# Spreading the later adaLN products of one decoder block over more of its mixer stage

## The chip, the cores and the metric

The kernel runs on one core of one Trainium2 chip. The metric is device time in microseconds (us), from runs of the whole kernel; lower is better. Each engine of the core (TensorE, called PE in the profile; VectorE, DVE; ScalarE, ACT; GpSimd, POOL; and SyncE, SP, which here only issues transfers) works through its own list of instructions in the order in which that list was written.

## The reference

The computation is one decoder block on 512 tokens of width 2048. A vector `c` gives six modulation vectors, two token mixers (eight pairs of RWKV-7 heads and four causal pooling groups) read one projection, their outputs are projected back, and a gated MLP with a short convolution follows. Cut to what matters here:

```python
c_act = silu(c)
mod = c_act @ w_ada + b_ada                       # 2048 x 12288: adaLN
sh1, sc1, gt1, sh2, sc2, gt2 = split(mod, 6)
h = rmsnorm(x, norm1_g) * (1 + sc1) + sh1
p = h @ w_in
y_rwkv = rwkv7_mixer(p[..., :3360], ...)          # 16 heads of 64, delta rule
y_pool = pool_mixer(p[..., 3360:], ...)           # windows 2, 4, 8, 16
x = x + gt1 * (concat(y_rwkv, y_pool) @ w_out)
h = rmsnorm(x, norm2_g) * (1 + sc2) + sh2
x = x + gt2 * conv_ffn(h, w_up, conv_w, conv_b, w_down)
return rmsnorm(x, norm_f_g)
```

`sh1` and `sc1` are needed before the projection. `gt1`, `sh2` and `sc2` (48 blocks of 128 values, "the later products") are needed only when the output projection is finished. `gt2` is computed much later and is not touched.

## The kernel before

All activations stand transposed, 128 features by 512 tokens to a tile. Every large product is written as three matmuls of split operands (`mm3`, L118 to L122): high by high, high by low, low by high. A weight tile of 128x512 is loaded into `wraw` (four buffers), ScalarE rounds it to `whi` (L113), VectorE subtracts to give `wlo` (L115), and TensorE makes 12 matmuls of 128x512 of it.

The mixer stage runs from about 160 us to 780 us. Its TensorE work is of two sorts. The projection tiles of later pairs (`win_pair`, `win_tile`; lines L120 to L122 writing `mm`) have no one waiting closely for them; they are called fillers below. The other sort is a chain per head pair: `stage_a` (decay, keys, then a small triangular solve that goes out to DRAM and back: L417 on TensorE, L420, L423, L427, L429 to L438 on VectorE, L443, L446, L449), `stage_b` (larger inverse blocks: L474 to L519) and `stage_c` (four chunks of the recurrence, L532 to L582, then normalisation and gate, L588 to L605). The loop over eight pairs emits fillers for pair p+2, `stage_a` of pair p+1, `stage_c` of pair p, and `stage_b` of pair p+1, the last three with high priority. After the loop come three pooling groups (1, 2, 0), each with a weight tile from `load_pw` (L271), projection tiles and `pool_front`/`pool_back` (L283 to L303), and then the output projection (`out_block`).

The order on each engine is not written out by hand: a scheduler of the framework takes instructions by priority (high-priority blocks first, else the order of the program) as its own model of time says that they become ready, and it also chooses the buffers.

The later products are made on VectorE, in `ada_rest`. Each of its 192 steps (48 blocks by 4 quarters of `c`) loads 256 KB into a tile `war` (L350, issued by SP), multiplies it with the broadcast quarter `cq`, and sums along the row into one column of `modq` (L351, which shows as a SCALAR_TENSOR_TENSOR and a short DVE_READ_ACCUMULATOR). They are called adaLN steps below. The tag `war` has three buffers, and the pooling weights of groups 1, 2 and 0 take theirs from the same three:

```python
    def load_pw(gi):
        t = ra.tile([P, T], F32, tag="war", name="pw", bufs=3) if gi < 3 else ring("pw")
        pw = t.rearrange("p (i d) -> p i d", i=2)
        nc.sync.dma_start(pw, a["poolw"][gi, :, :, :])
        return pw
```

A pooling weight keeps its buffer until `pool_back` of its group has run its matmuls (L298). L663 to L667 add the four quarters and make `mod` and `gsc2`, which are first read after the output projection.

Of the kernel before, what the change touches and what calls it, by code (L numbers as in the profile page):

```python
# [55 lines left out]
def block_kernel(ctx, tc, a, out, stop=None, dbg=None):  # L56
# [30 lines left out]
    def col(name, i):  # L87
        return vec[:, COLS[name] + i : COLS[name] + i + 1]
# [50 lines left out]
    def split_act(k, src):  # L139
        hi, lo = slots(k)  # L140
        S.copy(hi, src)
        V.tensor_tensor(lo, src, hi[:, :].bitcast(F32), op=ALU.subtract)
        return hi, lo
# [33 lines left out]
    if True:  # L177
# [53 lines left out]
        if True:  # L231
# [5 lines left out]
            def ring(name):  # L237
                return ring16(name)[:, 16:]

            def ring16(name):  # L240
                return ra.tile([P, 16 + T], F32, tag="ring", name=name, bufs=7)
# [26 lines left out]
# [6 lines that stand above are left out]
    def pool_front(gi):  # L274
        win = WINS[gi]
        zs = []
        for i in range(2):
            cur = upad[i]
            lo = 1
            step = 1  # L280
            while step < win:
                nxt = ring16("sw")
                V.tensor_add(nxt[:, lo:], cur[:, lo:], cur[:, lo - step : 16 + T - step])  # L283
                cur = nxt
                step *= 2
                lo += step
            z = ring("z")
            V.scalar_tensor_tensor(z, cur[:, 16:], 1.0 / win, upad[i][:, 16:], op0=ALU.mult, op1=ALU.subtract)
            V.tensor_mul(z[:, 0:win], cur[:, 16 : 16 + win], prec[:, 0:win])
            V.tensor_sub(z[:, 0:win], z[:, 0:win], upad[i][:, 16 : 16 + win])  # L290
            zs.append(z)
        return zs

    def pool_back(gi, zs, pw):
        for d in range(2):
            ps = atile()
            for i in range(2):
                PE.matmul(ps, pw[:, i, d * P : (d + 1) * P], zs[i], start=i == 0, stop=i == 1)  # L298
            j = gi * 2 + d
            mx = ring("mxp")  # L300
            S.activation(mx, ps, AF.Identity, bias=drv[:, 35 + j : 36 + j], scale=col("psc", j))
            if gi:
                nc.sync.dma_start(mixd[8 + j], mx)  # L303
            else:
                last_mix.append(split_act(14 + d, mx))
# [7 lines left out]
    def atile():  # L313
        return psa.tile([P, T], F32, tag="pa", name="pa", bufs=2)
# [8 lines left out]
    def win_tile(fi):  # L323
        ps = mmtile()
        project(ps, a["win1"][fi - 8, :, :], H)
        return ps
# [16 lines left out]
    def ada_rest(n0, n1):  # L343
        for n in range(n0, n1):
            kq, j = divmod(n, 48)
            if j == 0:
                cq[0] = ra.tile([P, T], F32, tag="cq", name="cq")
                nc.sync.dma_start(cq[0], cact[0:1, kq * T : (kq + 1) * T].partition_broadcast(P))
            wa = ra.tile([P, T], F32, tag="war", name="war", bufs=3)
            nc.sync.dma_start(wa, a["ada2"][kq, j, :, :])  # L350
            V.scalar_tensor_tensor(wa, wa, 1.0, cq[0], op0=ALU.mult, op1=ALU.mult,  # L351
                                   accum_out=modq[:, kq, j : j + 1])
# [256 lines left out]
    def win_pair(p):  # L609
        for i in range(3):  # L610
            ps = win_tile(8 + 3 * (p - 1) + i)
            t = ra.tile([P, T], F32, tag="spill", name="spill", bufs=2)
            shift(ps, 8 * i + p, t)
            d = tc.dram_tile([P, T], F32, name=f"sp{p}_{i}")
            nc.sync.dma_start(d, t)
            sp[p, i] = d

    def start_pair(p):
        if p:
            rkv = []  # L620
            for i in range(3):
                t = vtile("v") if i == 2 else ring("rkv")
                nc.sync.dma_start(t, sp[p, i])
                rkv.append(t)
        else:
            rkv = rkv0
        return stage_a(p, rkv)

    def hp():
        return tc.high_priority(offset=100000)  # L630
# [6 lines left out]
    for p in range(NP):  # L637
        if p + 1 < NP:
            if p + 2 < NP:
                win_pair(p + 2)  # L640
            with hp():
                qn = start_pair(p + 1)
        with hp():
            stage_c(p, q)
            if p + 1 < NP:
                stage_b(p + 1, qn)
                q = qn
        ada_rest(min(28 * p, 192), min(28 * p + 28, 192))
    last_mix = []
    for n, gi in enumerate((1, 2, 0)):  # L650
        pw = load_pw(gi)
        upad = []
        for i in range(2):
            ps = win_tile(29 + 2 * n + i)
            u = ring16("upad")
            V.memset(u[:, 0:16], 0.0)
            S.copy(u[:, 16:], ps)
            upad.append(u)
        if gi:
            with hp():  # L660
                pool_back(gi, pool_front(gi), pw)

    V.tensor_add(modq[:, 0, :], modq[:, 0, :], modq[:, 1, :])  # L663
    V.tensor_add(modq[:, 2, :], modq[:, 2, :], modq[:, 3, :])
# [489 lines left out]
    for f in range(NWF, KT):  # L1154
        n = f - NWF
# [111 lines left out]
```

## Time and profile before

| | us |
|---|---|
| median of 3 runs | 2364.33 (2362.54 to 2365.67) |
| the profiled execution, its time | 2367.32 |
| its span, first to last instruction | 2365.6 |
| TensorE busy | 2259.0 (95%) |
| VectorE busy | 1637.7 (69%) |
| ScalarE busy | 1066.4 (45%) |
| mean granted TensorE clock | 0.989 |

The page's chain of work that ended last is almost all TensorE. In the mixer stage TensorE is busy nearly all the time, but a busy TensorE there is partly one that runs small matmuls of the chain, and its order is fixed, so where one matmul's operand is late, all behind it wait. The rows to look at are therefore TensorE's idle time in that stage, what ended it, and the three lists (VectorE, SP, TensorE) around the adaLN steps.

### The profile page before, as it was taken

The page shows a single profiled execution, that of the slowest core. Times are in us where ns is not written, and L with a number is a line of the kernel's source. Part 1 is how long each engine was busy: PE and PEld are TensorE (multiplying, and loading weights), DVE is VectorE, ACT ScalarE, POOL GpSimd, SP SyncE. Part 2 cuts the span into 40 slices and gives each one's busy share as a digit, 9 for nine tenths or more (in the row PEclk, how much of TensorE's full clock was granted, in tenths as well). Part 3 has the DMA queues.
Part 4 walks back from the last instruction along what each step waited for, and adds up shares of the span by engine and source line. Part 5 has one row for each costly group of instructions (what it writes and reads, how often), then busy time and mean ns, then how long its engine had stood idle before and what let it go on. Part 6 is the DMA issues. An engine that isn't in the chain of part 4 may idle for free.

```text
span 2365.6 us, 42857 instructions
## 1 busy us (share of the span) xinstructions
PE 2259.0 (95%) x17122; PEld 1965.8 (83%) x17122; DVE 1637.7 (69%) x2591; ACT 1066.4 (45%) x1499; POOL 126.2 (5%) x185
## 2 busy tenths in 40 slices
PE   3879999999999999999999999999999999999997
PEld 2656666666666789999999999999999888888897
DVE  6987687777684456788888877777777645353354
ACT  3235253445433345665555555555555522233353
POOL 0000000000000000010101000000000000110000
PEclk9999999999999999999999999999999999999999
DMA  9976556566672756598888877777776767663464
GB/s 345 339 232 184 164 157 175 153 179 188 172 207 74 242 190 191 169 284 246 231 245 234 237 212 199 197 198 199 199 197 185 237 212 272 228 211 117 123 183 160
DMA packets 226234, 483.06 MB, mean 204 GB/s; under 512 B 74545, under 2 KB 79601, under 8 KB 217841
## 3 DMA queue, kind: packets, MB, share of 16 engines
q1 hardware_dynamic: 206114, 413.21, 54.5%
q0 software_dynamic: 18864, 66.07, 13.6%
q8 instruction: 134, 2.20, 0.4%
q10 hardware_dynamic: 1056, 1.05, 0.1%
q14 instruction: 66, 0.54, 0.1%
HBM read 441.70 MB, written 38.54 MB: 203 GB/s over the span
## 4 chain that ended last, share of the span: by engine, by line
PE 57%; issue 8%; DVE 1%; DMA 1%; ACT 1%; POOL 0%; POOLq 0%; DVEq 0%; ACTq 0%
PE b L122 18%; PE b L120 18%; PE b L121 18%; DMA wrow<-wup 1%; PE mm L122 1%; PE mm L121 1%; PE mm L120 1%; PE pb L122 0%; PE pa L122 0%; PE pa L120 0%; PE pa L121 0%; PE pb L120 0%; PE pb L121 0%; ACT x L787 0%; PE pa L298 0%
## 5 line engine op out<-in xcount | busy, mean ns | idle before, releaser
L122 PE MATMUL b<-t,ulo 128*128 128x256 f32 x1408 | 397.2, 282 | 0.0
L120 PE MATMUL b<-t,uhi 128*128 128x256 f32 x1408 | 396.8, 282 | 0.0
L121 PE MATMUL b<-t,uhi 128*128 128x256 f32 x1408 | 396.7, 282 | 0.0
L122 PE MATMUL b<-act,ulo 128*128 128x512 f32 (+1 forms) x880 | 308.0, 350 | 0.0
L121 PE MATMUL b<-act,uhi 128*128 128x512 f32 (+1 forms) x880 | 307.8, 350 | 0.0
L120 PE MATMUL b<-act,uhi 128*128 128x512 f32 (+1 forms) x880 | 307.7, 350 | 0.0
L120 PE MATMUL b<-y,uhi 128*128 128x256 f32 x1056 | 297.4, 282 | 2.7 <-ACT uhi L854 2.7
L122 PE MATMUL b<-y,ulo 128*128 128x256 f32 x1056 | 297.3, 282 | 0.5 <-DVE ulo L856 0.5
L121 PE MATMUL b<-y,uhi 128*128 128x256 f32 x1056 | 297.1, 281 | 0.0
L856 DVE TENSOR_TENSOR ulo<-wd,uhi 128x1024 fp32r<-128x1024 f32 (+1 forms) x120 | 136.3, 1136 | 217.9 <-ACT uhi L854 213.0
L113 ACT CAST whi<-wraw 128x512 fp32r<-128x512 f32 x236 | 145.5, 620 | 274.7 <-PE mm L121 115.3
L120 PEld LDWEIGHTS b<-t,uhi 128*128 128x128 f32 x1408 | 266.9, 190 | 0.0
L122 PEld LDWEIGHTS b<-t,ulo 128*128 128x128 f32 x1408 | 266.9, 190 | 0.0
L121 PEld LDWEIGHTS b<-t,uhi 128*128 128x128 f32 x1408 | 266.8, 190 | 0.0
L854 ACT CAST uhi<-wquart 128x1024 fp32r<-128x1024 f32 x156 | 164.0, 1052 | 202.6 <-PE b L121 176.2
L854 ACT CAST uhi<-wd 128x1024 fp32r<-128x1024 f32 (+1 forms) x120 | 117.6, 980 | 293.2 <-PE b L121 291.1
L856 DVE TENSOR_TENSOR ulo<-wquart,uhi 128x1024 fp32r<-128x1024 f32 x156 | 190.9, 1224 | 72.0 <-ACT uhi L854 72.0
L115 DVE TENSOR_TENSOR wlo<-wraw,whi 128x512 fp32r<-128x512 f32 x236 | 161.1, 688 | 100.3 <-ACT whi L113 92.6
L854 ACT CAST uhi<-r 128x1024 fp32r<-128x1024 f32 x132 | 138.8, 1051 | 163.2 <-PE b L121 161.3
L856 DVE TENSOR_TENSOR ulo<-r,uhi 128x1024 fp32r<-128x1024 f32 x132 | 161.3, 1222 | 61.9 <-ACT uhi L854 61.9
L120 PEld LDWEIGHTS b<-y,uhi 128*128 128x128 f32 x1056 | 199.6, 189 | 3.1 <-ACT uhi L854 3.1
L122 PEld LDWEIGHTS b<-y,ulo 128*128 128x128 f32 x1056 | 199.3, 189 | 0.9 <-DVE ulo L856 0.9
(314 smaller groups left out, 4719.0 us busy)
## 6 DMA issues: line engine op xcount, KB each, us to landing
wquart<-wup SPq DMA_DIRECT2D x176, 512.0 KB, 4.8
wa<-ada SPq DMA_DIRECT2D x48, 1024.0 KB, 6.9
war<-ada SPq DMA_DIRECT2D x192, 256.0 KB, 3.4
wd<-wdn SPq DMA_DIRECT2D x80, 512.0 KB, 3.8
wraw<-win SPq DMA_DIRECT2D x140, 256.0 KB, 4.1
wraw<-wout SPq DMA_DIRECT2D x96, 256.0 KB, 3.5
wquart<-wup POOLq DMA_DIRECT2D x44, 512.0 KB, 7.5
r<-wup SPq DMA_DIRECT2D x44, 512.0 KB, 4.6
```

What stands on the lines that cost most here:

```text
L113: S.copy(hi, raw)
L115: eng.tensor_tensor(lo, raw, hi[:, :].bitcast(F32), op=ALU.subtract)
L120: PE.matmul(ps, wh, xh, start=start, stop=False, skip_group_check=more)
L121: PE.matmul(ps, wh, xl, start=False, stop=False, skip_group_check=more)
L122: return PE.matmul(ps, wl, xh, start=False, stop=stop, skip_group_check=more)
L854: S.copy(hi[:, 0:n], src)
L856: lo_of[0] = V.tensor_tensor(lo[:, 0:n], src, hi[:, 0:n].bitcast(F32), op=ALU.subtract)
```

## The change

Two lines. Before, each of the first seven pairs emitted up to 28 adaLN steps after its `stage_c`, and pair 7 none. Now each of the eight pairs emits 18, and each of the three pooling groups after the loop emits 16 more.

```diff
-        ada_rest(min(28 * p, 192), min(28 * p + 28, 192))
+        ada_rest(18 * p, 18 * (p + 1))
     last_mix = []
     for n, gi in enumerate((1, 2, 0)):
         pw = load_pw(gi)
@@
         if gi:
             with hp():
                 pool_back(gi, pool_front(gi), pw)
+        ada_rest(144 + 16 * n, 160 + 16 * n)
```

The number of instructions of each kind is the same; their order differs on all engines from about pair 1 on.

VectorE, in the small solve of pair 7 (L435 and L437 are its steps, L351 the adaLN steps, L598 to L604 the end of pair 6's `stage_c`, L115 the split of a projection weight). Before:

```order
L351 SCALAR_TENSOR_TENSOR war,modq<-war,cq 128x512
L437 TENSOR_TENSOR xyl<-xyl,prod 64x7x8
L351 SCALAR_TENSOR_TENSOR war,modq<-war,cq 128x512
L435 TENSOR_TENSOR prod<-xyl,nl 64x56
L598 TENSOR_TENSOR rs<-y,rs 128x512
L437 TENSOR_TENSOR xyl<-xyl,prod 64x8x7
L351 SCALAR_TENSOR_TENSOR war,modq<-war,cq 128x512
L435 TENSOR_TENSOR prod<-xyl,nl 64x54
L600 TENSOR_TENSOR rs<-rs,bv 128x512
L437 TENSOR_TENSOR xyl<-xyl,prod 64x9x6
```

After, the same stretch:

```order
L351 SCALAR_TENSOR_TENSOR war,modq<-war,cq 128x512
L437 TENSOR_TENSOR xyl<-xyl,prod 64x7x8
L559 COPY U<-ch 128x128
L435 TENSOR_TENSOR prod<-xyl,nl 64x56
L115 TENSOR_TENSOR wlo<-wraw,whi 128x512
L437 TENSOR_TENSOR xyl<-xyl,prod 64x8x7
L435 TENSOR_TENSOR prod<-xyl,nl 64x54
L437 TENSOR_TENSOR xyl<-xyl,prod 64x9x6
L435 TENSOR_TENSOR prod<-xyl,nl 64x50
L351 SCALAR_TENSOR_TENSOR war,modq<-war,cq 128x512
```

Between L429 and L438 of pair 7 there are 14 adaLN steps before and 5 after; the end of pair 6 (L598, L600, L604) has moved behind the solve.

SP, at the end of the pairs (L271 loads a pooling weight, L605 stores the last pair's output, L111 loads projection weights). Before:

```order
L350 DMA war<-ada 128x512 x3
L111 DMA wraw<-win 128x512 x2
L271 DMA pw<-poolw 128x512 x2
L111 DMA wraw<-win 128x512 x3
L271 DMA pw<-poolw 128x512
L111 DMA wraw<-win 128x512 x5
L303 DMA mixd_110<-mxp 128x512
L303 DMA mixd_111<-mxp 128x512
L111 DMA wraw<-win 128x512
L605 DMA mixd_107<-rs 128x512
```

After, from the load of the last pooling weight on:

```order
L271 DMA pw<-poolw 128x512
L605 DMA mixd_107<-rs 128x512
L350 DMA war<-ada 128x512
L111 DMA wraw<-win 128x512 x2
L350 DMA war<-ada 128x512
L111 DMA wraw<-win 128x512
L350 DMA war<-ada 128x512
L111 DMA wraw<-win 128x512
L350 DMA war<-ada 128x512
L111 DMA wraw<-win 128x512
```

Before, the last adaLN load stands ahead of all three pooling weights; after, 48 adaLN loads stand behind the first of them, 32 behind the second and 16 behind the third, in turn with projection weights.

VectorE behind the last pair (L283 to L290 are pooling, L115 the splits that the fillers need). Before:

```order
L604 TENSOR_TENSOR rs<-rs,ch 128x512
L115 TENSOR_TENSOR wlo<-wraw,whi 128x512
L283 TENSOR_TENSOR sw<-upad 128x527
L283 TENSOR_TENSOR sw<-sw 128x525
L283 TENSOR_TENSOR sw<-sw 128x521
L115 TENSOR_TENSOR wlo<-wraw,whi 128x512
```

After, a few rows on in the same place:

```order
L351 SCALAR_TENSOR_TENSOR war,modq<-war,cq 128x512
L283 TENSOR_TENSOR sw<-sw 128x521
L115 TENSOR_TENSOR wlo<-wraw,whi 128x512
L288 SCALAR_TENSOR_TENSOR z<-sw,upad 128x512
L289 TENSOR_TENSOR z<-sw,prec 128x8
L290 TENSOR_TENSOR z<-z,upad 128x8
L351 SCALAR_TENSOR_TENSOR war,modq<-war,cq 128x512
L115 TENSOR_TENSOR wlo<-wraw,whi 128x512
```

Here every split of a projection weight now stands behind an adaLN step, and with it behind that step's load.

## Rows read from the trace of the kernel before

**Rows 1.** The page, part 1: busy us, share of the span, instructions.

```profile
PE 2259.0 (95%) x17122; PEld 1965.8 (83%) x17122; DVE 1637.7 (69%) x2591; ACT 1066.4 (45%) x1499; POOL 126.2 (5%) x185
```

**Rows 2.** Busy time by stretch (length, each engine, granted clock, DMA share, GB/s).

```profile
240.00:620.00 380.00, 368.91 (x3835) 254.89 (x3833) 288.61 (x743) 172.98 (x263) 0.00 (x0) 0.99 0.60 170
620.00:720.00 100.00, 91.57 (x1036) 66.76 (x1036) 75.61 (x198) 32.70 (x53) 0.00 (x0) 0.98 0.65 186
720.00:780.00 60.00, 59.17 (x358) 39.56 (x357) 27.27 (x54) 23.81 (x40) 0.00 (x0) 1.00 0.30 89
```

**Rows 3.** PE's waits, 240 to 800 us (us in total, times, longest).

```profile
PE pb L501 <- DVE Tm L498: 2.1, 2, 1.9
...
PE mm L122 <- DVE wlo L115: 0.8, 1, 0.8
...
PE pb L483 <- DVE Tm L477: 0.5, 1, 0.5
```

**Rows 4.** Tile `war`, whole span: its DVE instructions, DVE's waits.

```profile
L351 DVE SCALAR_TENSOR_TENSOR war<-war,cq x192: 673/683/695, 165.3 to 705.7; 128x512 f32<-128x512 f32 x192
L351 DVE DVE_READ_ACCUMULATOR war<-war,cq x192: 72/82/92, 165.9 to 706.3; 128x1 f32 x192
...
  DMA war<-ada: 20.5, 19
```

**Rows 5.** DVE's time on tile `war` alone, by stretch.

```profile
680.00:700.00 20.00, 8.17 (x23) 1.00 0.75 207
700.00:720.00 20.00, 2.11 (x8) 1.00 0.60 171
720.00:740.00 20.00, 0.00 (x0) 1.00 0.13 41
```

**Rows 6.** Timeline of pair 7's solve and two waits behind it (start, us).

```profile
667.15 0.41 DVE L429 TENSOR_TENSOR xyl<-nl,lanei 64x256 f32<-64x256 f32 x1
...
690.27 0.38 DVE L438 COPY xyl<-xyl 64x256 f32<-64x256 f32 x1
...
693.92 0.50 PE L122 MATMUL mm<-ah,wlo 128*128 128x512 f32 x1 [0.81 <-DVE wlo L115]
...
705.87 0.72 PE L483 MATMUL pb<-Tm,x 32*32 32x32 f32 x62 [0.52 <-DVE Tm L477]
```

**Rows 7.** Timeline: a solve's result arrives (L449), TensorE takes it (L474); pairs 5, 7.

```profile
553.10 0.61 ACT L449 COPY x<-x4l 128x512 f32<-128x512 f32 x1
...
554.37 0.75 PE L474 MATMUL pb<-x,nt 32*32 32x32 f32 x64
...
699.48 0.62 ACT L449 COPY x<-x4l 128x512 f32<-128x512 f32 x1 [2.06 <-DMA x4l<-dxz]
...
704.59 0.75 PE L474 MATMUL pb<-x,nt 32*32 32x32 f32 x64
```

**Rows 8.** A buffer of `war` changes hands; landing of such loads, 640 to 705 us.

```profile
698.19 0.69 DVE L351 SCALAR_TENSOR_TENSOR war<-war,cq 128x512 f32<-128x512 f32 x1
...
698.91 0.35 SPq L350 DMA_DIRECT2D war<-ada  x1
...
DMA to landing us min/median/max: 2.5/3.0/4.4
```

**Rows 9.** The end of pair 7, and two fillers in a row.

```profile
750.85 1.12 PE L603 MATMUL ch<-xg,lw 32*128 32x512 f32 x2
...
754.80 0.32 SPq L605 DMA_DIRECT2D mixd<-rs  x1
...
776.42 0.39 PE L121 MATMUL mm<-al,whi 128*128 128x512 f32 x1
...
777.55 0.39 PE L120 MATMUL pb<-ah,whi 128*128 128x512 f32 x1
```

**Rows 10.** VectorE's copies in two chunks of pair 7's `stage_c`.

```profile
727.52 0.29 DVE L559 COPY U<-ch 128x128 f32<-128x128 f32 x1 [2.10 <-PE ch L557]
...
732.44 0.29 DVE L559 COPY U<-ch 128x128 f32<-128x128 f32 x1 [2.18 <-PE ch L557]
```

**Rows 11.** All engines in 20 us with a lower granted clock (columns as in rows 2).

```profile
620.00:640.00 20.00, 16.18 (x309) 12.36 (x308) 13.14 (x29) 5.06 (x8) 0.00 (x0) 0.91 0.62 188
```

## The prediction, made before the changed kernel ran

> **What bounds the kernel now.** I read the page first. TensorE is busy for 2259.0 of 2365.6 us and VectorE for 1637.7 [rows 1], so a change of VectorE's order can only move the end through TensorE's idle time. All that the change moves lies in the mixer stage, so the busy time by stretch came next. From the place where the two orders part, in pair 1 at about 240 us, to the end of the stage, TensorE is idle for 380 - 368.91 = 11.1, then 100 - 91.57 = 8.4, then 60 - 59.17 = 0.8 us: 20.3 us in all [rows 2]. That is all there is to win, and most of it was never the adaLN steps' doing. PE's waits over the same time say which part is: eight rows name a VectorE instruction, from 2.1 us down to 0.5 us, and sum to 8.6 us [rows 3]; the rest name ScalarE or nothing ("issue").
>
> Then the adaLN steps themselves. A step costs VectorE 0.683 + 0.082 = 0.765 us, 192 steps 147 us, and VectorE waited 20.5 us in 19 pieces (1.1 us each) for their loads [rows 4]. They end at 706 us: VectorE spends 8.17 of 20 us on them just before, and nothing from 720 us on, where it is busy for only 27.27 of 60 us [rows 2, 5]. So the change takes work from a stretch where VectorE is 76% busy to one where it is 45% busy. That reads like a gain, and the question is how much of it TensorE sees.
>
> **How much really moves.** The diff speaks of 28 steps a pair becoming 18, but the scheduler had already delayed them. Counted in VectorE's list, 191 steps stand ahead of L477 of pair 7 before and 162 after. Over the eight pairs that is some 24 a pair becoming 20: 29 steps, 22 us of VectorE, go behind pair 7's solve.
>
> **Pair 7's solve: shorter, and covered less.** Before, from L429 to the end of L438 it takes 690.65 - 667.15 = 23.5 us [rows 6], with 14 adaLN steps in between. After, 5 stand there. Gone are 9 steps (6.9 us) and, all of 128x512 and so about 0.69 us like the multiply of a step [rows 4], three weight splits, the three operations that end pair 6 and three pooling operations (6.2 us). One copy, one masking and one update of pair 6's chunks come in; I put 1.5 us on them, an estimate from the 0.29 us of a copy [rows 10] and some 0.9 for the masking. The solve gets 11.6 us shorter. But TensorE's list between L417 and L474 of that pair holds 75 fillers where it held 128. A filler takes (777.55 - 776.42) / 5 = 0.226 us [rows 9], so TensorE arrives 53 x 0.226 = 12.0 us sooner. Before, the result was there at 699.48 + 0.62 = 700.1 and TensorE came at 704.59: 4.5 us to spare [rows 7]. After: 4.5 + 11.6 - 12.0 = 4.1. No new wait, and no gain from the shorter solve either; TensorE's work is only put in another order. What can go are the two waits on VectorE next to it, 0.81 and 0.52 us [rows 6]: **-1.3**.
>
> **Pairs 1 to 6.** Their solves hold nearly the same number of steps as before (10 and 9 in pair 3, 11 and 10 in pair 5). Pair 5 loses cover most: 102 fillers become 93, 2.0 us. It had 554.37 - 553.71 = 0.7 us to spare [rows 7], and what leaves its solve (one step, the end of pair 4: 2.8 us) is matched by what enters (two maskings, a copy, two updates: about 2.8 us). So a wait of up to 1.4 us can arise at L474 of pair 5. The nine fillers stand elsewhere and may cover another wait, so the ends are 0 and 1.4; I take the upper one, since I see no place that needs them: **+1.4**.
>
> **The shared buffers.** This is what the change adds without saying so. The pooling weights live in the adaLN steps' three buffers. Before, all three pooling weights were loaded after the last step. After, the second is loaded while the first is held, and the third while the second is held: adaLN steps 161 to 169 and 177 to 182 have one buffer, the others from 145 on two. With one buffer a step's load can be issued only when the step before has read its tile, and the load's time lies open. Such a trip is 3.0 us from issue to landing (2.5 to 4.4), 0.68 for the multiply, and 0.04 for the hand-over (the multiply ends at 698.87, the next load goes out at 698.91): **3.7 us**, between 3.2 and 5.1 [rows 8, 4]. VectorE and SP work in order, so behind a waiting step stand VectorE's splits of projection weights, and behind a waiting load SP's loads of them; TensorE waits for both.
>
> The Trainium skill has a rule against this, in "DMA: Bandwidth & Descriptors", section "Rules for kernel authors": issue a transfer early, compute, and wait for it late, so that its fixed cost is hidden. Rows 8 show the fixed cost (2.5 us at best for 256 KB). The same page's fit for one transfer (section "Anatomy of one DMA", measured on GpSimd's path) gives an estimate of 2.0 + 0.6 = 2.6 us, a trip of 3.3 us, and by it the sum below would lose its +0.8 at the tail; no run here shows that path.
>
> *Steps 161 to 169* lie beside `stage_b` and `stage_c` of pair 7. A chunk of `stage_c` takes 732.44 - 727.52 = 4.9 us, and VectorE sits idle for 2.1 us in it ahead of its copy [rows 10]. One step stands in each chunk; at 3.7 us a trip its data is there, and its 0.77 us fit the idle time. Bounds: 0, and 3 us (two waits of 1.1 us as in rows 4, and 0.2 a chunk at 5.1 us a trip). The first is nearer: **+0.5**.
>
> *Steps 177 to 182* are the tight place. Count from the start of pair 7's L603 on TensorE. The store L605 follows 754.80 - 750.85 = 3.95 us later [rows 9], and the load of step 177 goes out at 4.3. Six trips end at 4.3 + 6 x 3.7 = 26.5, and the split behind step 182 is done at 27.3. TensorE needs it for its 116th filler from there, at 1.05 + 116 x 0.226 + 2.2 (two pairs of pooling matmuls, about 1.1 us each, as L603's 1.12) = 29.5. So there are 2.2 us to spare over six trips: they may take 4.07 us each, a landing of 3.35. The ten steps behind have two buffers, so 3.7 / 2 = 1.9 us a step and 19 us in all, beside the splits of six weight tiles of 12 x 0.226 = 2.7 us, 16 us: they lose 3 us, of which the 2.2 us to spare cover most. Bounds: 0, and at the slowest landing 6 x (5.1 - 4.07) = 6.2 us. DMA there is lighter (30% of the engines' time, against 65% [rows 2]), so the landing should be at or under the median, and I take what is left, 3 - 2.2: **+0.8**.
>
> **The end.** `mod` and `gsc2` come some 75 us later than the 706 us of before, at about 785 us. They are first read when the first eight output tiles are done, 8 x 4 weight tiles of 2.7 us = 87 us behind the first matmul of the output projection (the last of rows 9, at 777.55), so near 865 us. Those 80 us hide it; it would cost only what passes them.
>
> **The sum** against the profiled execution: -1.3 + 1.4 + 0.5 + 0.8 = +1.4 us on 2367.3. That execution lies 3.0 us above the median of the runs, so against the median: 2364.3 + 1.4 = 2365.7, say **2366 us**. A measurement of this kernel can tell about 0.2%, 4.7 us, from no change.
>
> **The rivals.**
> - *One buffer starves TensorE (slower).* Place: steps 177 to 182, on TensorE at the first matmul that reads the late split. It decides where a trip is over 4.07 us. For it: single landings reach 4.4 us, and here SP also takes turns with projection loads. Price: 6.2 us; and where TensorE had stood for 3.8 us in 20, the granted clock in those 20 us was 0.91 of the higher level (a stretch at 1.2 GHz), which costs another 0.09 x 20 = 1.8 us [rows 11]. 2365.7 - 0.8 + 6.2 + 1.8 = 2373 us in full, 2370 with half of it. Chance 0.22.
> - *Relief (faster).* VectorE was what TensorE waited for, and with fewer steps in the pairs these waits go. All eight rows are 8.6 us [rows 3]; that two thirds of them vanish and nothing comes back gives 2364.3 - 5.7 = 2358.6 us. Against it: four of every five steps stay where they were. Chance 0.13.
> - *The change does not do what it says.* The scheduler had spread the steps by itself, so that the new numbers only shuffle fillers: 2364 us, within the noise. Chance 0.20, on the same side as the forecast.
>
> **How the numbers follow.** The forecast has 0.45. It and the third rival lie within 0.2%: same 0.65, slower 0.22, faster 0.13. The range runs from 2358 (the relief in two thirds) to 2373 (the starved TensorE in full), which leaves out less than 2 in 10.
>
> **What would show it.** After, the tile `war` should show VectorE waiting for its loads more often than 19 times, with most of it behind 690 us, and last steps at about 780 us. PE's waits between 740 and 790 us should stay at 1 to 2 us: if they name `wlo` (L115) with several us, the first rival holds. L474 of pair 7 should come about 4 us after its L449, and L474 of pair 5 should show a wait of 1 to 2 us. TensorE's idle time from 240 us to the first matmul of the output projection should be 20 to 23 us. The forecast is wrong if that idle time falls under 15 us (the adaLN steps were TensorE's wait after all) or passes 26 us; and wrong in its reason if the time stays but a trip on one buffer is over 4.1 us.

## The result, and the profile after

| | before | after |
|---|---|---|
| median, us (7 runs each, in turn) | 2363.41 (2358.32 to 2367.11) | 2370.88 (2368.21 to 2374.57) |
| ratio, with its 95% interval | | 1.0026 [1.0016, 1.0036] |
| the profiled execution, us | 2367.32 | 2368.21 |

The changed kernel is slower by about 6 us, 0.26% by the ratio (the medians alone stand 7.5 us apart). That lies inside the range, but on the side I had given 0.22, not on the "no change" of the forecast. The two profiled executions don't show this loss at first sight: that of before is slower than all its seven runs, that of after is the fastest of its own, and they differ by 0.9 us.

The page of after, part 1 (busy us, share of the span, instructions), answers [rows 1]:

```profile
PE 2258.3 (95%) x17122; PEld 1963.7 (83%) x17122; DVE 1640.5 (69%) x2591; ACT 1063.9 (45%) x1499; POOL 126.0 (5%) x185
```

Both engines do the same work as before to within 0.2%. The busy time by stretch answers [rows 2] (columns: stretch, length, busy PE, PEld, DVE, ACT, POOL, granted clock, DMA share, GB/s):

```profile
240.00:620.00 380.00, 365.51 (x3817) 251.57 (x3817) 285.93 (x735) 171.29 (x261) 0.00 (x0) 0.98 0.59 164
620.00:720.00 100.00, 95.90 (x1117) 68.42 (x1115) 67.79 (x161) 35.06 (x58) 0.00 (x0) 1.00 0.53 142
720.00:780.00 60.00, 57.34 (x295) 39.80 (x291) 36.44 (x88) 21.91 (x35) 0.00 (x0) 1.00 0.58 178
```

TensorE's idle time has changed places: 14.5, 4.1 and 2.7 us where it was 11.1, 8.4 and 0.8. The sum is 21.3 us against 20.3. VectorE's work has moved to the last stretch, as meant: 36.4 us there instead of 27.3. The tile `war` answers [rows 4]:

```profile
L351 DVE SCALAR_TENSOR_TENSOR war<-war,cq x192: 652/684/694, 166.0 to 789.0; 128x512 f32<-128x512 f32 x192
...
  DMA war<-ada: 30.2, 30
...
DMA to landing us min/median/max: 2.4/3.5/6.4
```

VectorE now waits 30.2 us for these loads instead of 20.5, and the last step starts at 789 us instead of 706. All of that was expected. PE's waits, 240 to 800 us, answer [rows 3] (us in total, times, longest):

```profile
PE mm L121 <- issue: 4.8, 2, 2.6
PE pb L514 <- DVE y L508: 4.3, 4, 1.6
PE ch L602 <- ACT rs L596: 2.4, 3, 1.3
PE pa L298 <- DVE z L290: 2.2, 2, 1.4
...
PE mm L120 <- issue: 0.9, 1, 0.9
```

No row names the split `wlo` (L115) any more, and the two waits that I had counted as won are gone. Instead there are waits at L121, L514 and L602 that before did not have, or had smaller. None of these rows names an adaLN step; that one of the waits still hangs on a step's load is shown under "Where the time goes".

### The profile page after: what moved, and what is told of

Its sections match the earlier page's. It is cut to its first block, busy times and chain, and to the rows that moved or that the text cites. A ratio compares the mean times of both kernels' runs of the same rounds, so it can differ in the third digit from the quotient of the medians.

```text
span 2366.4 us, 42856 instructions
## 1 busy us (share of the span) xinstructions
PE 2258.3 (95%) x17122; PEld 1963.7 (83%) x17122; DVE 1640.5 (69%) x2591; ACT 1063.9 (45%) x1499; POOL 126.0 (5%) x185
## 4 chain that ended last, share of the span: by engine, by line
PE 83%; DVE 7%; DMA 4%; ACT 3%; issue 2%; SPq 0%; DVEq 0%; ACTq 0%
PE b L122 20%; PE b L120 20%; PE b L121 20%; PE mm L121 4%; PE mm L122 4%; PE mm L120 4%; DVE jk L212 2%; DMA war<-ada 1%; PE pb L541 1%; DMA wrow<-wup 1%; PE pb L539 1%; PE pa L298 1%; DMA wraw<-win 1%; DVE wlo L115 1%; PE pa L532 1%
## 5 line engine op out<-in xcount | busy, mean ns | idle before, releaser
L121 PE MATMUL b<-t,uhi 128*128 128x256 f32 x1408 | 396.7, 282 | 0.0
L121 PE MATMUL b<-act,uhi 128*128 128x512 f32 (+1 forms) x880 | 307.8, 350 | 0.0
L121 PE MATMUL b<-y,uhi 128*128 128x256 f32 x1056 | 297.7, 282 | 0.0
L121 PEld LDWEIGHTS b<-t,uhi 128*128 128x128 f32 x1408 | 266.8, 190 | 0.0
L115 DVE TENSOR_TENSOR wlo<-wraw,whi 128x512 fp32r<-128x512 f32 x236 | 161.1, 687 | 86.2 <-ACT whi L113 81.4
```

What stands on the lines that cost most here:

```text
L115: eng.tensor_tensor(lo, raw, hi[:, :].bitcast(F32), op=ALU.subtract)
L121: PE.matmul(ps, wh, xl, start=False, stop=False, skip_group_check=more)
```

## The experiments

Each kernel ran in turn with the kernel before on the same chip, 5 to 12 runs each against 26 to 33 of before. The ratio is to before, with its 95% interval.

**The measurement's own floor: both kernels again (before_again, after_again).** No edit.

> The kernel before once more, for its spread, the granted clock of each of its runs and a second trace. It should lie within 2 us of the kernel before (2363.4 us). Theory 'one buffer' (the change's loss of 6 to 7 us is waiting on the shared war buffers): granted clock like that of the changed kernel's seven runs, 0.987 to 0.990, mean 0.9887. Theory 'clock' (the new order has more stretches at half the clock): mean clock here 0.990 to 0.992, since 0.001 of the mean clock is 2.4 us of the span.

> The changed kernel once more, for a second trace beside the second one of before. 2369 to 2372 us, ratio 1.0016 to 1.0036. Theory 'one buffer': this trace shows TensorE idle 3 us or more longer between 740 and 790 us than before, with waits that name wlo (L115) or pooling (L290). Theory 'clock': idle time in the mixer stage within 2 us of before's, and more time at the lower clock between 240 and 780 us.

The kernel before against itself gave 1.0012 [1.0001, 1.0024]. The changed kernel gave 1.0026 [1.0011, 1.0041], 2367.30 against 2360.07 us. So the loss comes back, and any ratio within 0.12% of 1 means nothing here.

**The shared buffers taken away (pw_spill).** The pooling weights of the changed kernel move to another tag, so that the steps always have three buffers:

```diff
-        t = ra.tile([P, T], F32, tag="war", name="pw", bufs=3) if gi < 3 else ring("pw")
+        t = ra.tile([P, T], F32, tag="spill", name="pw", bufs=2) if gi < 3 else ring("pw")
```

> The changed kernel with the three pooling weights in the two buffers of tag spill, which are free by then, so that adaLN steps always have their three buffers. Theory 'one buffer': the loss goes, 2362 to 2366 us. Theory 'clock' or 'new order' (fillers stand elsewhere in the pairs): stays at 2368 to 2372 us.

2367.43 us, 1.0030 [1.0016, 1.0044]: nothing comes back. My main rival falls, and the time shows nothing of my own +0.5 and +0.8.

**The steps taken out (no_ada).** Before without its 192 later adaLN steps, so that `gt1`, `sh2` and `sc2` are only their biases:

```diff
-        ada_rest(min(28 * p, 192), min(28 * p + 28, 192))
+    G.memset(modq, 0.0)
```

> The kernel before without its 192 later adaLN steps (loads and multiplies left out, the sums set to zero, so gt1, sh2 and sc2 are only their biases). It bounds what any placement of the steps can win. If TensorE waits for VectorE because of the steps: 2355 to 2359 us. If its waits are of another sort: 2361 to 2365 us.

2358.55 us, 0.999 [0.9981, 0.9999]. Without all 147 us of VectorE work the end comes some 2 us sooner, hardly more than the floor, and the loss of 6 us is larger. I had meant this run as a bound on what any placement can win. It is none: taking the steps out makes a new list too, and 24 steps a pair (below) come out no slower with all of them in.

**The tail half of the change alone (tail_only).** 28 steps a pair until 144 are done, then 16 for each pooling group:

```diff
-        ada_rest(min(28 * p, 192), min(28 * p + 28, 192))
+        ada_rest(min(28 * p, 144), min(28 * p + 28, 144))
@@
+        ada_rest(144 + 16 * n, 160 + 16 * n)
```

> The other half: 28 steps a pair until 144 are made, and 16 in each pooling group. Theory 'place of the steps' (the tail is at fault): 2366 to 2369 us. Theory 'order': another draw, 2358 to 2369 us.

2362.86 us, 1.0000 [0.9989, 1.0010]: steps among the pooling weights, shared buffers included, cost nothing that shows in the time.

**An even spread over the eight pairs alone (pairs_only, pairs_again).** 24 a pair, none in the groups, measured twice:

```diff
-        ada_rest(min(28 * p, 192), min(28 * p + 28, 192))
+        ada_rest(24 * p, 24 * (p + 1))
```

> Half of the change: 24 steps for each of the eight pairs, none in the pooling groups. Theory 'place of the steps' (the tail is at fault): 2359 to 2363 us. Theory 'order': another draw of the scheduler, anywhere from 2358 to 2369 us, and its time says nothing of the tail.

> 24 steps for each of the eight pairs and none in the groups, a second time. The first gave 0.9986 [0.9976, 0.9996], while the kernel before run against itself gave 1.0012. If the gain is real: 0.9980 to 0.9993, about 2359 us. If it was scatter of the measurement: 0.9993 to 1.001.

0.9986 [0.9976, 0.9996] and, on another chip, 0.9982 [0.9968, 0.9995] (2359.47 us). This is the best version of this study, and it beats both kernels: before by 3 to 5 us, twice just outside the floor, and so the changed one by some 10 us. A more even spread is thus not bad in itself.

**The pair half of the change alone (pairs18_only).** 18 a pair, all the rest with pair 7:

```diff
-        ada_rest(min(28 * p, 192), min(28 * p + 28, 192))
+        ada_rest(18 * p, 18 * (p + 1) if p < 7 else 192)
```

> The other half of the change alone: 18 steps for each of pairs 0 to 6 as in the changed kernel, and all the rest (66) after pair 7, none in the pooling groups. TensorE's list is the changed kernel's word for word up to the small solve of pair 6 (about 620 us) and another one behind. If the loss of about 6 us is made in pairs 1 to 5 (idle time behind the larger solves and a stretch at 1.2 GHz near 582 us, both reproduced there in two traces of the changed kernel): 2366 to 2369 us, ratio 1.002 to 1.0035, and a stretch at 1.2 GHz of about 10 us near 580 us. If it is made behind pair 6: 2360 to 2364 us, ratio 0.999 to 1.001. If the shared buffers at the end mattered (already unlikely): no loss either, since no step stands between pooling weights here.

2370.71 us, 1.0023 [1.0011, 1.0035]: the whole loss, with no step in the groups. With the tail half's 1.0000 the loss goes with the 18 a pair and not with the steps in the groups. The order behind pair 6 is a new one here too, so this run doesn't say in which pair the loss is made.

**The same idea with other numbers (neighbour_20).** 20 a pair, then 11, 11 and 10:

```diff
-        ada_rest(18 * p, 18 * (p + 1))
+        ada_rest(20 * p, 20 * (p + 1))
@@
-        ada_rest(144 + 16 * n, 160 + 16 * n)
+        ada_rest(160 + 11 * n, min(171 + 11 * n, 192))
```

> The same idea with other numbers: 20 steps for each of the eight pairs and 11, 11 and 10 for the pooling groups, in place of 18 and 16. Its list on TensorE leaves the changed kernel's in pair 2 (about 265 us). If spreading the steps this way costs by itself (steps in pairs 5 to 7 and among the pooling weights), it comes out like the changed kernel: 2366 to 2370 us, ratio 1.002 to 1.004. If the loss belongs to the one order that the scheduler made of 18 and 16, this is another draw and may fall anywhere from pairs_only to the changed kernel: 2358 to 2368 us, and more likely within 0.15% of the kernel before, 2360 to 2366.

2365.29 us, 1.0005 [0.9991, 1.0018]. The neighbour doesn't show the loss. It is no other draw, as I had expected it to be: up to pair 6 its lists are the changed kernel's (see below).

**Order and steps taken apart.** A function stores the permutation that the scheduler made of one kernel, and adds order-only edges between successive instructions of TensorE, VectorE, ScalarE and SP. The adaLN steps, their loads and the pooling weights' loads stay free:

```python
for engine, order in ORDERS.items():
    seq = [i for i in done if on(i, engine) and i.name not in floating]
    for x, y in zip(order[:-1], order[1:]):
        tc.add_manual_dep(seq[y], seq[x].name, NoSync)
```

In steps_moved_only the changed kernel's steps should run beside the order of before; in order_moved_only the steps of before beside the changed kernel's order. The scheduler places the free steps anew, so the copies are not exact: ahead of L477 of pair 7 stand 171 and 192 steps, against 162 after and 191 before; ahead of L477 of pair 6 stand 151 and 168, against 147 after and 150 before.

> The changed kernel, with the order of every other instruction of the stage on TensorE, VectorE, ScalarE and SP held to that of the kernel before; only the adaLN steps, the broadcasts of c, the final sums and the three pooling weights float. Theory 'order' (the loss comes from the fillers and chain steps that the scheduler set in another order): the loss goes, 2359 to 2363 us. Theory 'place of the steps' (it comes from where the steps themselves and their loads stand): it stays, 2366 to 2369 us.

> The mirror: the kernel before, with 28 steps a pair, and the order of everything else held to that of the changed kernel. Theory 'order': the loss is here without the change, 2365 to 2369 us. Theory 'place of the steps': 2359 to 2363 us.

2369.54 us, 1.0034 [1.0021, 1.0047], and 2380.95 us, 1.0075 [1.0062, 1.0088]. Both mixtures lose, and the changed kernel's order with the steps of before loses most. They do not separate the two theories. Up to pair 6 steps_moved_only has the order of before and nearly its step places, and loses all the same; and no kernel was run pinned to its own order, so what the pinning itself costs is not known. That an order fits the step positions it was made for is a guess that these runs leave open.

## Where the time goes

TensorE's lists sort these kernels. From 160 us to L474 of pair 6 (near 620 us, some 4,140 matmuls), after, pw_spill, pairs18_only and neighbour_20 have the same list but for at most 3 matmuls: list A. Before and tail_only have the same but for 5: list B. Between A and B at least 370 matmuls stand in another place. The 24-a-pair kernel has a third, C. So one order was traced several times, on different chips.

The busy time of two stretches, from L474 of pair 1 to L474 of pair 6, and from there to the first matmul of the output projection (columns as above; length less PE's busy time is TensorE's idle time). List B, before and tail_only:

```profile
284.10:620.09 335.99, 327.51 (x3313) 224.62 (x3312) 261.22 (x674) 163.44 (x244) 0.00 (x0) 0.99 0.61 171
620.09:777.55 157.46, 148.21 (x1380) 104.27 (x1380) 101.01 (x249) 55.40 (x91) 0.00 (x0) 0.99 0.51 149
```

```profile
280.82:616.33 335.51, 326.61 (x3309) 223.93 (x3308) 260.12 (x671) 162.96 (x244) 0.00 (x0) 0.99 0.61 170
616.33:774.34 158.01, 149.69 (x1384) 105.82 (x1384) 100.28 (x239) 55.33 (x91) 0.00 (x0) 0.99 0.50 145
```

List A, after, pairs18_only and neighbour_20:

```profile
280.83:627.52 346.69, 333.00 (x3318) 228.28 (x3317) 261.38 (x670) 163.47 (x245) 0.00 (x0) 0.98 0.60 165
627.52:779.66 152.14, 145.38 (x1370) 101.96 (x1370) 100.46 (x240) 54.30 (x90) 0.00 (x0) 1.00 0.52 149
```

```profile
283.18:628.23 345.05, 331.61 (x3319) 227.49 (x3318) 261.80 (x672) 163.53 (x245) 0.00 (x0) 0.99 0.61 165
628.23:786.51 158.28, 151.63 (x1370) 107.11 (x1370) 102.61 (x252) 54.81 (x91) 0.00 (x0) 0.96 0.51 153
```

```profile
284.69:626.86 342.17, 327.47 (x3319) 223.78 (x3318) 261.58 (x672) 163.41 (x245) 0.00 (x0) 1.00 0.61 167
626.86:776.79 149.93, 145.84 (x1370) 103.19 (x1370) 102.68 (x252) 54.63 (x91) 0.00 (x0) 1.00 0.55 160
```

List C, the second run of 24 a pair, and the kernel without the steps:

```profile
278.86:612.97 334.11, 325.51 (x3314) 222.75 (x3313) 259.30 (x670) 162.67 (x244) 0.00 (x0) 1.00 0.62 171
612.97:766.37 153.40, 149.03 (x1375) 105.34 (x1374) 103.32 (x254) 55.20 (x91) 0.00 (x0) 0.98 0.53 159
```

```profile
279.11:617.26 338.15, 326.78 (x3302) 222.97 (x3301) 197.88 (x442) 164.07 (x246) 0.00 (x0) 1.00 0.32 81
617.26:774.75 157.49, 153.30 (x1392) 107.76 (x1392) 77.42 (x162) 55.66 (x92) 0.00 (x0) 0.98 0.29 80
```

In the first stretch list B idles 335.99 - 327.51 = 8.5 us and list A 346.69 - 333.00 = 13.7 us. The granted clock of a stretch also counts: below 1.00 a part of it ran at 1.2 GHz. The table has the idle time of all kernels, and what the clock took: length x (1 - granted clock), summed over the seven stretches from L474 of pair 1 to the next L474 and so on to the output projection (the clock is given in hundredths, so this column is good to about half a microsecond).

| kernel, list | idle to pair 6 | idle behind | clock | sum | time against before, us |
|---|---|---|---|---|---|
| before, B | 8.5 | 9.3 | 3.7 | 21.5 | 0 |
| before_again, B | 8.3 | 8.6 | 3.1 | 20.0 | +2.5 |
| tail_only, B | 8.9 | 8.3 | 3.4 | 20.6 | -0.2 |
| after, A | 13.7 | 6.8 | 6.6 | 27.1 | +7.5 |
| after_again, A | 12.8 | 6.0 | 6.2 | 25.0 | +7.2 |
| pw_spill, A | 12.4 | 5.9 | 8.3 | 26.6 | +7.4 |
| pairs18_only, A | 13.4 | 6.7 | 12.1 | 32.2 | +6.5 |
| neighbour_20, A | 14.7 | 4.1 | 0.0 | 18.8 | +1.0 |
| pairs_only, C | 11.0 | 4.3 | 3.5 | 18.8 | -2.8 |
| pairs_again, C | 8.6 | 4.4 | 3.1 | 16.1 | -4.8 |
| no_ada, its own | 11.4 | 4.2 | 3.7 | 19.3 | -1.5 |
| steps_moved_only, B pinned | 11.5 | 9.5 | 3.4 | 24.4 | +6.4 |
| order_moved_only, A pinned | 17.7 | 5.7 | 17.3 | 40.7 | +17.9 |

The middle columns come from one execution each (that of pairs18_only was the slowest of its 12), the last from the medians. All the same, the sum orders the kernels nearly as the time does. Three things stand in it.

*List A has about 5 us more idle time in pairs 1 to 6.* Five traces give 12.4 to 14.7, three of list B 8.3 to 8.9; they don't overlap. The amount of VectorE work is not the reason: it is 261.38 us after and 261.22 before, and the kernel without the steps, with a list of its own and 261.22 - 197.88 = 63 us less of it, still idles 11.4 us. Pinned, list B idles 11.5 us with nearly the same steps ahead, so the list alone does not set the idle time. The places repeat. PE's waits from L474 of pair 3 to L474 of pair 5, before:

```profile
PE mm L120 <- issue: 1.7, 1, 1.7
```

after:

```profile
PE mm L121 <- issue: 2.6, 1, 2.6
PE ch L602 <- ACT rs L596: 1.9, 2, 1.3
PE mm L120 <- issue: 0.9, 1, 0.9
```

Neighbour_20 has the same three rows (2.6, 1.9 and 0.9 us in total). A filler behind the batch L483 of pair 4 waits 2.6 us instead of 1.7 ("issue": the profile shows no releaser), and L602, the gate of pairs 3 and 4, now waits 1.9 us in two pieces, by the profile for ScalarE's L596. In list B it has no such wait here.

*Behind pair 6 list A idles less*, 4.1 to 6.8 us instead of 8.3 to 9.3. In after the waits of before at L483, L539 and L460 and for `wlo` are gone there.

*The clock.* Four of the five traces of list A lose 6.2 to 12.1 us to stretches at 1.2 GHz, those of list B 3.1 to 3.7. They stand beside the chains of pairs 4 to 7; all four traces have one at about 490 us. What TensorE did ahead of the longest of after is in these rows:

```profile
562.00:572.00 10.00, 8.04 (x82) 5.83 (x81) 7.65 (x16) 5.84 (x8) 0.00 (x0) 0.98 0.50 163
572.00:582.00 10.00, 10.00 (x56) 7.67 (x56) 5.92 (x12) 1.71 (x3) 0.00 (x0) 0.51 0.18 53
```

From 562 to 572 us it stands for 2.0 of 10 us (1.55 of them at L514, behind VectorE's L508), and in the next 10 us the granted clock is 0.51, the lower level nearly all the time: 4.9 us lost. In neighbour_20, with the same list:

```profile
562.00:572.00 10.00, 8.38 (x100) 6.19 (x99) 8.19 (x17) 7.05 (x9) 0.00 (x0) 1.00 0.71 220
572.00:582.00 10.00, 9.55 (x83) 6.98 (x81) 9.23 (x18) 3.10 (x5) 0.00 (x0) 1.00 0.32 81
```

It stood for 1.6 us, in another place (L399, behind ScalarE's L397), and kept the full clock. Of the other traces of list A in these two stretches pairs18_only stood for 2.4 us (busy 7.60) and lost 3.4 us, pw_spill and the changed kernel's second trace stood for 0.7 and 0.4 us and lost nothing there. So the two that idled most lost the clock, the other three did not. Idle time alone does not decide, though: before stood for 1.9 of 10 us and 1.2 of the next 7.2, and kept the full clock.

```profile
635.00:645.00 10.00, 8.09 (x55) 5.75 (x54) 6.28 (x14) 4.58 (x7) 0.00 (x0) 1.00 0.64 198
645.00:652.20 7.20, 5.98 (x33) 3.65 (x31) 5.88 (x13) 4.28 (x6) 0.00 (x0) 1.00 0.39 109
```

How long TensorE stands from 562 to 572 us hangs on when loads land. In after VectorE stood 1.88 us for an adaLN step's load ahead of L508, and TensorE then 1.55 us for L508. In the second trace of the same kernel the same step waited 0.26 us, and L514 found its operand there. After:

```profile
567.25 0.69 DVE L351 SCALAR_TENSOR_TENSOR war<-war,cq 128x512 f32<-128x512 f32 x1 [1.88 <-DMA war<-ada]
...
570.68 1.21 PE L514 MATMUL pb<-x,nt 64*64 64x64 f32 x16 [1.55 <-DVE y L508]
```

after_again:

```profile
569.03 0.69 DVE L351 SCALAR_TENSOR_TENSOR war<-war,cq 128x512 f32<-128x512 f32 x1 [0.26 <-DMA war<-ada]
...
572.48 1.14 PE L514 MATMUL pb<-x,nt 64*64 64x64 f32 x16
```

In pairs18_only and neighbour_20 it was the reload of a spilled projection tile (`rkv`): ScalarE's L397 stood 3.17 and 2.39 us for it, and TensorE's L399 then 2.40 and 1.62 us for L397. So the place of an adaLN step's load did cost TensorE time here, in one execution of five. The second trace of the changed kernel loses it later:

```profile
562.00:572.00 10.00, 9.64 (x106) 7.19 (x105) 9.26 (x19) 8.37 (x10) 0.00 (x0) 1.00 0.74 240
572.00:582.00 10.00, 9.54 (x85) 6.72 (x84) 9.41 (x17) 2.21 (x4) 0.00 (x0) 1.00 0.31 86
650.00:660.00 10.00, 10.00 (x71) 6.58 (x69) 5.11 (x10) 3.00 (x6) 0.00 (x0) 0.73 0.74 196
```

The list makes the idle places; how long TensorE stands in each differs between executions with the landing of loads, and where the clock falls differs too.

Together, after against before: about +5 idle to pair 6, -2.5 behind it, +3 for the clock, 5.5 of the measured 6 to 7 us. That the first pair of profiles hid this has one place too. Between L474 of pairs 0 and 1, ahead of these stretches, the profiled execution of before lost 3.5 us to the clock and 2.6 to idling, that of after 0 and 0.8. Before:

```profile
245.21:284.10 38.89, 36.27 (x501) 26.23 (x500) 22.82 (x50) 7.85 (x16) 0.00 (x0) 0.91 0.61 176
```

after:

```profile
246.25:280.83 34.58, 33.78 (x505) 24.37 (x505) 22.49 (x48) 7.82 (x16) 0.00 (x0) 1.00 0.66 189
```

Other executions of both kernels have it the other way round (before_again 0 and 1.5 us, after_again 3.5 and 2.2): four of the five traces of list A lose 3.5 us to the clock there, and one of the three of list B. So the first pair of profiles is an unlucky draw and no gain. With this stretch taken in, the way from L474 of pair 0 to the output projection takes 531.8 to 542.8 us in list A (mean 536.4) and 527.4 to 532.3 us in list B (mean 529.9): 6.4 us apart, the whole measured loss.

**What stays open.** Neighbour_20 has list A and its idle time, but hardly loses. From 160 us to L474 of pair 6 its order is the changed kernel's on TensorE, VectorE, ScalarE and SP, adaLN steps included, but for at most 4 instructions of an engine. So the 5 us of idle time in pairs 1 to 6 do not make the loss by themselves, and the two kernels part behind pair 6: there the lists differ, neighbour_20 idles least, and its trace has no stretch at 1.2 GHz behind L474 of pair 1. How much of that is its order and how much the one execution that was traced is not known. Nor is it shown why list A makes TensorE stand longer at L121, where the profile names no releaser.

## Why the prediction was right or wrong

- **Pairs 1 to 6, +1.4: the step that failed.** I looked only at the slack of the solves, and put the cost at L474 of pair 5. There is none. The rows that answer [rows 7] (pair 5, then pair 7):

```profile
551.12 0.62 ACT L449 COPY x<-x4l 128x512 f32<-128x512 f32 x1
...
553.37 0.32 PE L474 MATMUL pb<-x,nt 32*32 32x32 f32 x15
...
689.91 0.62 ACT L449 COPY x<-x4l 128x512 f32<-128x512 f32 x1
...
692.41 0.38 PE L474 MATMUL pb<-x,nt 32*32 32x32 f32 x22
```

  Pair 5's result is there at 551.12 + 0.62 = 551.7, TensorE comes 1.6 us later. In its place about 5 us of idle time arose at L121, L602 and L514 (L399 in other executions of the list). That the new list had moved filler work away from operands that were not ready is my reading; no run shows it apart from the rest. "I see no place that needs them" was said of nine fillers; I had looked up neither the other batches nor ScalarE.
- **Pair 7's solve, -1.3: right in sign, too small.** The solve, L429 to the end of L438, was mis-sized:

```profile
663.20 0.41 DVE L429 TENSOR_TENSOR xyl<-nl,lanei 64x256 f32<-64x256 f32 x1
...
677.76 0.37 DVE L438 COPY xyl<-xyl 64x256 f32<-64x256 f32 x1
```

  It takes 678.13 - 663.20 = 14.9 us, 8.6 less than the 23.5 of before, where I had 11.6 less. TensorE comes 1.9 us behind the end of L449 (690.53), where the sum had 4.1, and finds the result there. The two waits of [rows 6] are gone, and behind pair 6 the idle time fell by 2.5 us in all.
- **The shared buffers, +0.5 and +0.8: the trip right, its price not seen in the time.** Steps 177 to 182 on VectorE (start, us; in brackets the wait and its releaser):

```profile
746.58 0.68 DVE L351 SCALAR_TENSOR_TENSOR war<-war,cq 128x512 f32<-128x512 f32 x1
...
749.93 0.69 DVE L351 SCALAR_TENSOR_TENSOR war<-war,cq 128x512 f32<-128x512 f32 x1 [1.78 <-DMA war<-ada]
...
753.33 0.69 DVE L351 SCALAR_TENSOR_TENSOR war<-war,cq 128x512 f32<-128x512 f32 x1 [0.29 <-DMA war<-ada]
...
758.50 0.69 DVE L351 SCALAR_TENSOR_TENSOR war<-war,cq 128x512 f32<-128x512 f32 x1 [1.40 <-DMA war<-ada]
...
761.84 0.69 DVE L351 SCALAR_TENSOR_TENSOR war<-war,cq 128x512 f32<-128x512 f32 x1 [0.41 <-DMA war<-ada]
...
765.37 0.69 DVE L351 SCALAR_TENSOR_TENSOR war<-war,cq 128x512 f32<-128x512 f32 x1 [2.17 <-DMA war<-ada]
```

  Five trips take 765.37 - 746.58 = 18.8 us, 3.76 each: four of 3.3 to 3.5 us and one of 5.2. I had 3.7 and a bound of 4.07. The Trainium skill's page "DMA: Bandwidth & Descriptors" (section "Anatomy of one DMA") gave an estimate of 2.6 us for such a landing. Most of the step loads from 744 to 762 us agree with it, though SyncE issued them:

```profile
DMA to landing us min/median/max: 2.6/2.6/4.4
```

  One in four took 4.4 us, and all 192 have a median of 3.5, so the mean of the trips came out as [rows 8] had it. (GpSimd's own loads, which I had said no run shows, are in the trace of before: 44 of 512 KB, 7.5 us from issue to landing at the median.) TensorE did stand for the long trip. The pooling operations behind its step (758.50) came late with it, and L298 waited for them:

```profile
761.48 1.98 PE L298 MATMUL pa<-z,pw 128*128 128x512 f32 x4 [1.45 <-DVE z L290]
```

  Pw_spill has no such wait, but one of 2.0 us at L496 in the same stage, and is no faster; tail_only shows no cost either.
- **The first rival** (2373 us, 0.22) gave a time nearer to the measured one, but its mechanism pays nothing in pw_spill, so that was luck. *Relief*: taking all the steps out gives some 2 us, not the 5.7 of its sum. *The change does not do what it says* was nearest in its reading (the numbers shuffle fillers) and wrong that shuffling is free.
- **The clock** stood in the sum of one rival only, as 1.8 us behind an idle stretch [rows 11]. In the forecast it was nothing. In the two traces compared above it is 3 us, half of the loss; by the mean clocks of all executions (0.9893 in the second measurement of the changed kernel, 0.9902 of before beside it) it is 0.0009 x 2367 = 2 us, a third.
- **The signs that I named** came but for the two at L474: 30 waits for `war`, last steps at 789 us, waits of 2.2 us on pooling (L298) and none on `wlo`, 21.3 us idle where I had said 20 to 23. They could not catch the loss, because one profiled execution of before stood 4 us above its median.

## What to carry to other kernels

When a scheduler makes the order, an edit of some steps is a new order of everything: compare the whole list of the bounding engine, and look at each displaced batch for what its operand waits on, not only at the batches that the edit was about. If the moved work costs little even when it is taken out altogether, the reshuffle becomes the main term, in either direction (here 1.003 with 18 and 16, 0.998 with 24 a pair); try a few neighbouring numbers and keep the best. Where an order is pinned, run the kernel pinned to its own order too. Where the loss is a quarter of a percent, read several traces of the same kernel before a place is named.

## What the runs showed of the hardware

The mean granted clock of a whole run goes with its time: the changed kernel's runs go from 2359.95 to 2374.57 us and their clocks from about 0.992 to 0.987, and order_moved_only, the slowest, has 0.985 where before has 0.990. I had not expected a short idle time to cost more by the clock than by itself: 2.0 us of standing were followed by 10 us at a granted 0.51, 4.9 us lost, while the same list of matmuls kept the full clock in executions that stood for 0.4 and 1.6 us there, and before kept it behind 1.9 us of standing at 635 to 645 us.
